# The first projection block of a two-layer decoder trunk traced piece by piece, with its loads issued in the order of their use

## The chip, the cores and the metric

The kernel runs on one core of a Trainium2 chip. The metric is device time in microseconds (us) of one execution; lower is better. The engines are PE (TensorE, the matrix multiplier; PEld is its weight load), DVE (VectorE), ACT (ScalarE), POOL (GpSimd) and SP (SyncE, which here only issues DMA transfers).

## The reference

The input is x, 256 tokens by 2048 channels, float32. Layer 0 mixes tokens by a gated linear recurrence (HGRN2), layer 1 by a gated spatial MLP; after each mixer stands a gated feed-forward network with a short causal convolution. Every sub-layer ends in `x = LayerNorm(ALPHA * x + sublayer(x))`. The part that matters here is the very first projection:

```python
proj = x @ w_in                       # (256 x 2048) @ (2048 x 8192)
q, f, i, g = split(proj)              # 2048 columns each
q = silu(q)
```

The first block of the kernel computes the first 512 columns of q, out of the whole of x and 512 columns of w_in.

## The kernel before

**Splitting.** Every matmul operand that needs float32 accuracy is held as two tiles, hi (the value rounded to fp32r) and lo (the remainder). A product takes hi times hi, hi times lo and lo times hi. For an activation tile X both halves lie side by side, 256 columns each, so that in `block_b` one matmul of 512 columns (`both`, L159: weight hi against X hi and X lo) and one of 256 columns (`rest`, L166: weight lo against X hi) do one product of 128 rows by 128 columns. Such a couple is called a pair below.

**Weights.** `plan` lists all weight chunks in the order of use. A chunk is 512 by 512 floats (1 MB, four slices of 128 rows). `fetch` (L73) issues its load on SP into one of three `raw` buffers; `convert` (L83) makes `whi` with ACT (L93) and `wlo` with DVE (L94), by default in two halves of two slices. `chunk` keeps up to AHEAD = 3 chunks in progress. A load into a `raw` buffer waits until the chunk three places earlier has been converted.

**The first block.** x lies in memory by tokens and has to be turned: `turn(t, k0, n)` (L299) transposes n slices of 128 channels of token tile t on PE into `pt`, copies them to X hi with ACT and subtracts with DVE into X lo (both L317). Two PSUM buffers serve all `pt` tiles. The main program walks over XSEQ: five pieces of x, of 2, 2, 4, 4 and 4 slices of 128 channels. For each piece it issues the load of x, the load of a weight chunk (the first one in four pieces of 256 KB, all four ahead of the second piece of x), then the two turns, under `tc.high_priority()`, and then the conversion of the chunk, ordered after the turns by `issue_after`. Only then does `hgrn` begin, whose first `block_b` call writes the matmuls: 4 chunks of 16 pairs, for each slice k of x four pairs j = 0 to 3 into four PSUM tiles `pb`. In the last chunk the pairs run by j.

**What sets the order.** A scheduler in the recording layer merges all this into one fixed sequence for each engine when the program is built: an earlier place in the program gives priority, `high_priority()` raises it, `issue_after` is a lower bound. On the chip each engine works through its sequence and waits on semaphores.

In the text below, x0 to x4 are the five pieces of x, and chunk 0 to chunk 3 the four weight chunks of the first block. x0 and x1 belong to chunk 0, and x2, x3, x4 to chunks 1, 2, 3.

Of the kernel before, what the change touches and what calls it, by code (L numbers as in the profile page):

```python
# [8 lines left out]
F32 = mybir.dt.float32  # L9
# [6 lines left out]
P = 128  # L16
S = 256
D = 2048
NK = D // P
# [6 lines left out]
NB = 512  # L26
CK = 4
# [3 lines left out]
AHEAD = 3  # L31
# [2 lines left out]
PAD_LO = 128  # L34
PAD1 = 224
BLOCK = {1: 32, 4: 32, 16: 64}
XSEQ = ((0, 2, 4), (2, 2, 0), (4, 4, 1), (8, 4, 1), (12, 4, 0))
TURN_ACT = 3


class Trunk:
# [28 lines left out]
    def want(self, w, k0, c0, extra=False):  # L70
        self.plan.append((w, k0, c0, extra))

    def fetch(self, pieces=1):  # L73
        w, k0, c0, extra = self.plan[self.issued]
        self.issued += 1
        raw = self.wp.tile([P, CK, NB], F32, tag="raw", name="raw")
        src = w[k0 * P : (k0 + CK) * P, c0 : c0 + NB].rearrange("(k p) n -> p k n", p=P)
        n = CK // pieces
        for i in range(0, CK, n):
            self.nc.sync.dma_start(raw[:, i : i + n, :], src[:, i : i + n, :])  # L80
        return raw, extra

    def convert(self, raw, extra, pieces=2):  # L83
        nc = self.nc
        pool = self.xp if extra else self.wp
        hi = pool.tile([P, CK, NB], F32R, tag="hi", name="whi")
        if not extra:
            pool.tile([P, PAD_LO], mybir.dt.uint8, tag="gap", name="gap", bufs=1)
        lo = pool.tile([P, CK, NB], F32R, tag="lo", name="wlo")
        n = CK // pieces  # L90
        for i in range(0, CK, n):
            s = slice(i, i + n)
            nc.scalar.copy(hi[:, s, :], raw[:, s, :])  # L93
            self.last_lo = nc.vector.tensor_tensor(  # L94
                lo[:, s, :], raw[:, s, :], hi[:, s, :].bitcast(F32), ALU.subtract
            )
        self.ready.append((hi, lo))

    def ahead(self, n):
        while self.issued < min(self.taken + n, len(self.plan)):  # L100
# [46 lines left out]
            for t in range(2):  # L147
                evac(t, ps[t])

    def block_b(self, act, w, nch, c0, evac, halves=False):  # L150


        nc = self.nc
        ps = [self.acc.tile([P, 2, S], F32, tag="acc", name="pb") for _ in range(4)]
        last = nch * CK - 1

        def both(ch, k, j, s=slice(0, S), start=True):
            c = slice(j * P, (j + 1) * P)
            nc.tensor.matmul(  # L159
                ps[j][:, :, s], ch[0][:, k % CK, c], act[:, k, :, s],  # L160
                start=start and k == 0, stop=k == last, skip_group_check=halves,
            )

        def rest(ch, k, j):
            c = slice(j * P, (j + 1) * P)
            nc.tensor.matmul(  # L166
                ps[j][:, 1, :], ch[1][:, k % CK, c], act[:, k, 0, :],
                start=False, stop=False, skip_group_check=halves,
            )

        def one(ch, k, j):
            for m in (rest, both) if k else (both, rest):
                m(ch, k, j)

        first = 0
        if halves:
            first = nch
            held = [self.chunk(w, ci * CK, c0) for ci in range(nch)]
            for t in range(2):
                for k in range(last):  # L180
                    for j in range(4):
                        both(held[k // CK], k, j, slice(t * P, (t + 1) * P), t == 0)
            for k in range(last):
                for j in range(4):
                    rest(held[k // CK], k, j)
            for j in range(4):
                one(held[-1], last, j)
        for ci in range(first, nch):
            ch = self.chunk(w, ci * CK, c0)
            ks = range(ci * CK, (ci + 1) * CK)  # L190
            if ci < nch - 1:
                order = [(k, j) for k in ks for j in range(4)]
            else:
                order = [(k, j) for j in range(4) for k in ks]
            for k, j in order:
                one(ch, k, j)
        for j in range(4):
            evac(j, ps[j])

    def gather(self, pool, ps, out):  # L200

        nc = self.nc
        r = pool.tile([P, S], F32, tag="rest", name="rest")
        nc.scalar.copy(r, ps[:, 1, :])  # L204
        nc.vector.tensor_tensor(out, ps[:, 0, :], r, ALU.add)
# [212 lines left out]
    def masks(self, h1):  # L418
# [25 lines left out]
        for i in range(4):  # L444
            s = slice(32 * i, 32 * i + 32)
            nc.gpsimd.tensor_copy(self.diag[s], self.ident[s, s])

    def hgrn(self):
        nc, tc = self.nc, self.tc
        w = self.a["hg_w_in"][0]  # L450
        with ExitStack() as st:
            hp = st.enter_context(tc.tile_pool(name="hp", bufs=1))
            lp = st.enter_context(tc.tile_pool(name="lp", bufs=2))
            h1 = st.enter_context(tc.tile_pool(name="h1", bufs=1))
            self.load_vectors(h1.tile([P, 8, P], F32, tag="o", name="rows"))
            self.masks(h1)
            scores = []
            for i in range(2):
                sc = [
                    h1.tile([P, *n], F32, name=f"{name}{i}")  # L460
                    for name, n in (("scores", (3, 2, P)), ("near32", (4, 32)), ("near64", (4, 64)))
                ]
                for s in sc:
                    nc.gpsimd.memset(s, 0.0)
                scores.append(sc)
            for g in range(4):
                self.hgrn_group(g, w, hp, lp, h1, scores)

    def hgrn_group(self, g, w, hp, lp, h1, scores):
        nc = self.nc  # L470
        q = hp.tile([P, 4, S], F32, tag="q", name="q")
# [5 lines left out]
        def ev_silu(dst):  # L477
            def ev(j, ps):
                self.gather(lp, ps, dst[:, j, :])
                r = lp.tile([P, S], F32, tag="sig", name="sig")  # L480
                nc.scalar.activation(r, dst[:, j, :], AF.Sigmoid)
                nc.vector.tensor_tensor(dst[:, j, :], dst[:, j, :], r, ALU.mult)

            return ev
# [10 lines left out]
        def ev_v(t, ps):  # L495
            nc.scalar.copy(v[:, t, :], ps)

        self.block_b(self.X, w, 4, 0 * D + g * NB, ev_silu(q))
        if g == 0:
            self.vectors()  # L500
            self.bounds(h1)
# [12 lines left out]
        for half in range(2):  # L514
            ps = self.misc.tile([P, 2, 2, P], F32, tag="m", name="po")
            for t in range(2):
                for hh in range(2):
                    i = half * 4 + t * 2 + hh
# [4 lines left out]
            for hh in range(2):  # L523
                j = 2 * half + hh
# [308 lines left out]
@with_exitstack  # L833
def tile_trunk(ctx: ExitStack, tc: tile.TileContext, *args):
    a = dict(zip(_INS, args))
    out = args[len(_INS)]
    k = Trunk(ctx, tc, a)
    nc = tc.nc
    k.plan_hgrn()
    k.plan_ffn(0)  # L840
    k.plan_gmlp()
    k.plan_ffn(1)
    k.constants()
    for k0, n, pieces in XSEQ:
        k.load_x(k0, n)
        chunk = k.fetch(pieces) if pieces else None
        with tc.high_priority():
            for t in range(2):
                hi, lo = k.turn(t, k0, n)
        if chunk:  # L850
            with tc.issue_after(hi.ins), tc.issue_after(lo.ins):
                k.convert(*chunk, pieces=max(pieces, 2))
    k.hgrn()

    def store(t, c):
        s = slice(c * NB, (c + 1) * NB)
        nc.sync.dma_start(out[0, t * P : (t + 1) * P, s], k.z[:, t, s])

    k.hgrn_out()
    k.ffn(0)  # L860
    k.xps.close()
    k.gmlp()
    k.ffn(1, store)
    k.xps.close()
    k.ln.close()
# [32 lines left out]
```

## Time and profile before

| what | value |
|---|---|
| three runs | 2281.47 us median (2280.64 to 2282.81) |
| the profiled execution: its own time | 2282.26 us |
| its span in the trace | 2280.6 us |
| PE busy in the span | 2258.8 us, 12781 matmuls |
| DVE, ACT busy | 1473.4 us, 1105.4 us |
| bytes read from memory | 425.98 MB, 188 GB/s over the span |
| first matmul of the first block, first one of the second block | 9.83 us, 36.99 us from the span's start |

The span runs from the first to the last recorded instruction; the run's own time is 1.7 us longer. An engine's busy time says little alone: what counts is which engine the chain of work that ended last runs through, and where that engine stands idle. In a timeline, the number in brackets is the idle time ahead of a row and the name behind the arrow what ended it. Neighbouring matmuls overlap in the records, since the end of one is drawn after the start of the next; their pace is read from the distance of their starts.

### The profile page before, as it was taken

Reading aid. Unit: us, or ns where it says so; the run is one execution under the profiler, and the core shown is the slowest. Engines: PE = TensorE matmul, PEld = TensorE weight load, DVE = VectorE, ACT = ScalarE, POOL = GpSimd, SP = SyncE. Lnnn points to the kernel's source line nnn. Section 1 sums busy time; section 2 is a strip of 40 time slices with the busy share of each in tenths; the row PEclk is TensorE's granted clock in tenths of the full one; section 3 lists DMA queues with packets and bytes.
Section 4 is the critical chain, followed back from the end, with each engine's and each line's share of the span. In section 5 each row is a group of like instructions: output and inputs, shape, how many; then the busy total and the mean of one; then the engine's idle time right before and its main releaser. Section 6 shows DMA issues by size and latency. Waiting matters only on the chain.

```text
span 2280.6 us, 31751 instructions
## 1 busy us (share of the span) xinstructions
PE 2258.8 (99%) x12781; PEld 1925.7 (84%) x12781; DVE 1473.4 (65%) x2327; ACT 1105.4 (48%) x1698; POOL 48.5 (2%) x102
## 2 busy tenths in 40 slices
PE   8999999999999999999999999999999999999998
PEld 7888888889888888888888888888888888888886
DVE  5777677667665665456666676566765666465655
ACT  5666565545443444344444545455444444344542
POOL 3000000000000000000000000000000000000000
PEclk9999999999999999999999999999999999999999
DMA  7454645645565555555555676655565555555563
GB/s 260 151 181 140 198 149 167 206 166 200 186 227 196 186 185 187 199 186 185 187 196 175 208 218 183 230 177 181 185 234 180 196 186 193 193 185 187 183 203 111
DMA packets 214052, 430.14 MB, mean 189 GB/s; under 512 B 7544, under 2 KB 8336, under 8 KB 213904
## 3 DMA queue, kind: packets, MB, share of 16 engines
q1 hardware_dynamic: 209536, 415.26, 54.5%
q0 software_dynamic: 4368, 12.85, 1.9%
q8 instruction: 100, 1.64, 0.3%
q14 instruction: 48, 0.39, 0.0%
HBM read 425.98 MB, written 2.10 MB: 188 GB/s over the span
## 4 chain that ended last, share of the span: by engine, by line
PE 97%; DVE 2%; ACT 1%; DMA 0%; issue 0%; SPq 0%; DVEq 0%; ACTq 0%
PE pb L159 38%; PE pb L166 20%; PE pa L123 12%; PE pa L125 12%; PE pa L124 12%; DVE wlo L94 1%; PE pl L550 1%; PE pt L305 1%; ACT whi L93 0%; PE pg L752 0%; PE pa L673 0%; PE pa L675 0%; PE pa L674 0%; DMA z<-in_x_dram 0%; PE po L522 0%; PE pout L642 0%
## 5 line engine op out<-in xcount | busy, mean ns | idle before, releaser
L94 DVE TENSOR_TENSOR wlo<-raw,whi 128x1024 fp32r<-128x1024 f32 (+1 forms) x786 | 930.6, 1219 | 693.3 <-ACT whi L93 684.9
L159 PE MATMUL pb<-X,whi 128*128 128x512 f32 (+1 forms) x3960 | 1335.1, 388 | 1.9 <-DVE X L317 1.9
L93 ACT CAST whi<-raw 128x1024 fp32r<-128x1024 f32 (+1 forms) x786 | 790.2, 1047 | 894.8 <-PE pb L159 418.7
L166 PE MATMUL pb<-X,wlo 128*128 128x256 f32 x3840 | 1049.7, 281 | 0.0
L159 PEld LDWEIGHTS pb<-X,whi 128*128 128x128 f32 x3960 | 725.0, 188 | 160.1 <-DVE X L317 2.3
L166 PEld LDWEIGHTS pb<-X,wlo 128*128 128x128 f32 x3840 | 715.7, 189 | 6.1
L123 PE MATMUL pa<-whi,Y 128*128 128x512 f32 x928 | 365.4, 394 | 0.0
L125 PE MATMUL pa<-whi,Y 128*128 128x512 f32 x928 | 363.5, 392 | 0.0
L124 PE MATMUL pa<-wlo,Y 128*128 128x512 f32 x928 | 361.2, 389 | 0.0
L125 PEld LDWEIGHTS pa<-whi,Y 128*128 128x128 f32 x928 | 173.9, 187 | 40.4
L124 PEld LDWEIGHTS pa<-wlo,Y 128*128 128x128 f32 x928 | 174.3, 188 | 37.8
L123 PEld LDWEIGHTS pa<-whi,Y 128*128 128x128 f32 x928 | 174.9, 188 | 35.6
L204 ACT COPY rest<-pb 128x256 f32<-128x256 f32 x240 | 87.9, 369 | 110.9 <-PE pb L159 92.9
L123 PE MATMUL pa<-whi,X 128*128 128x512 f32 x256 | 101.8, 398 | 0.0
L124 PE MATMUL pa<-wlo,X 128*128 128x512 f32 x256 | 101.4, 396 | 0.0
L125 PE MATMUL pa<-whi,X 128*128 128x512 f32 x256 | 100.6, 393 | 0.0
L803 DVE SCALAR_TENSOR_TENSOR act<-a,cols,act 128x254 f32<-128x254 f32 (+1 forms) x176 | 73.2, 481 | 0.0
L125 PEld LDWEIGHTS pa<-whi,X 128*128 128x128 f32 x256 | 48.1, 188 | 11.8
L123 PEld LDWEIGHTS pa<-whi,X 128*128 128x128 f32 x256 | 48.1, 188 | 11.4
L124 PEld LDWEIGHTS pa<-wlo,X 128*128 128x128 f32 x256 | 48.2, 188 | 10.6
L397 DVE TENSOR_TENSOR z<-z,pa 128x512 f32<-128x512 f32 x40 | 27.4, 684 | 34.5 <-PE pa L125 30.3
L807 ACT ACTIVATE act<-act 128x256 f32<-128x256 f32 x88 | 33.8, 415 | 8.7 <-DVE act L803 8.5
(164 smaller groups left out, 1033.2 us busy)
## 6 DMA issues: line engine op xcount, KB each, us to landing
raw<-in_ffn_w_up_dram SPq DMA_DIRECT2D x176, 1024.0 KB, 4.9
raw<-in_ffn_w_down_dram SPq DMA_DIRECT2D x88, 1024.0 KB, 4.9
raw<-in_hg_w_in_dram SPq DMA_DIRECT2D x63, 1024.0 KB, 5.1
raw<-in_sg_w_in_dram SPq DMA_DIRECT2D x32, 1024.0 KB, 5.5
raw<-in_hg_w_out_dram SPq DMA_DIRECT2D x16, 1024.0 KB, 4.9
raw<-in_sg_w_out_dram SPq DMA_DIRECT2D x16, 1024.0 KB, 4.9
g<-in_ln_g_dram POOLq DMA_DIRECT2D x16, 256.0 KB, 6.5
b<-in_ln_b_dram POOLq DMA_DIRECT2D x16, 256.0 KB, 8.8
```

The source lines that it names most:

```text
L93: nc.scalar.copy(hi[:, s, :], raw[:, s, :])
L94: self.last_lo = nc.vector.tensor_tensor(lo[:, s, :], raw[:, s, :], hi[:, s, :].bitcast(F32), ALU.subtract)
L123: nc.tensor.matmul(ps[t], xh, hi[:, kk, :], start=n[t] == 0, stop=False)
L124: nc.tensor.matmul(ps[t], xh, lo[:, kk, :], start=False, stop=False)
L125: nc.tensor.matmul(ps[t], xl, hi[:, kk, :], start=False, stop=last)
L159: nc.tensor.matmul(ps[j][:, :, s], ch[0][:, k % CK, c], act[:, k, :, s], start=start and k == 0, stop=k == last, skip_group_check=halves,)
L166: nc.tensor.matmul(ps[j][:, 1, :], ch[1][:, k % CK, c], act[:, k, 0, :], start=False, stop=False, skip_group_check=halves,)
L204: nc.scalar.copy(r, ps[:, 1, :])
L305: nc.tensor.transpose(ps[:, j, :], self.z[:, t, k * P : (k + 1) * P], self.ident)
L397: nc.vector.tensor_tensor(zz, zz, ps, ALU.add)
L803: nc.vector.scalar_tensor_tensor(cv[:, d:], x[:, : S - d], self.c(("cw", l, 2 - d), f), cv[:, d:], ALU.mult, ALU.add,)
L807: nc.scalar.activation(cv, cv, AF.Silu)
```

## The change

The main loop over XSEQ becomes a method `start`. `fetch` and `convert` are cut into a part that allocates and a function that does one piece, so that both can be called piece by piece. SP now issues x0, two slices of chunk 0, x1, the other two slices of chunk 0, and then x2, chunk 1, x3, chunk 2, x4. The turns of a piece lose `high_priority()` and get a lower bound instead: not before the matmuls of the first half of the piece before. The conversions still follow the turns of their piece. The matmuls of chunks 0 to 2 are written right behind the turns and conversions of each piece, instead of in `block_b`, which is left with chunk 3 (`begun`).

```diff
-XSEQ = ((0, 2, 4), (2, 2, 0), (4, 4, 1), (8, 4, 1), (12, 4, 0))
+XSEQ = ((0, 2), (2, 2), (4, 4), (8, 4), (12, 4))
...
+    def start(self):
+
+        tc = self.tc
+        self.load_x(*XSEQ[0])
+        first, load = self.begin_fetch()
+        load(0, 1)
+        load(1, 1)
+        self.load_x(*XSEQ[1])
+        load(2, 1)
+        load(3, 1)
+        raw = [first]
+        for x in XSEQ[2:]:
+            self.load_x(*x)
+            if len(raw) < 3:
+                raw.append(self.fetch())
+        ps = self.begun = self.begin_b()
+        last = None
+        for i, (k0, n) in enumerate(XSEQ):
+            with tc.issue_after(last.ins) if last else nullcontext():
+                for t in range(2):
+                    hi, lo = self.turn(t, k0, n)
+            c = k0 // CK
+            if c == 3:
+                break
+            if k0 % CK == 0:
+                step = self.begin_convert(*raw[c])
+            with tc.issue_after(hi.ins), tc.issue_after(lo.ins):
+                for m in range(0, n, n // 2):
+                    step(k0 % CK + m, n // 2)
+            for k in range(k0, k0 + n):
+                for j in range(4):
+                    ch = self.ready[c]
+                    if k:
+                        self.rest(ps, self.X, ch, k, j)
+                    m = self.both(ps, self.X, ch, k, j, NK - 1)
+                    if not k:
+                        m = self.rest(ps, self.X, ch, k, j)
+                if k == k0 + n // 2 - 1:
+                    last = m
+        self.ready = self.ready[3:]
+        self.taken = 3
+        with tc.issue_after(hi.ins), tc.issue_after(lo.ins):
+            self.ahead(AHEAD)
...
-        self.block_b(self.X, w, 4, 0 * D + g * NB, ev_silu(q))
+        self.block_b(self.X, w, 4, 0 * D + g * NB, ev_silu(q), begun=self.begun if g == 0 else None)
...
-    for k0, n, pieces in XSEQ:
-        k.load_x(k0, n)
-        chunk = k.fetch(pieces) if pieces else None
-        with tc.high_priority():
-            for t in range(2):
-                hi, lo = k.turn(t, k0, n)
-        if chunk:
-            with tc.issue_after(hi.ins), tc.issue_after(lo.ins):
-                k.convert(*chunk, pieces=max(pieces, 2))
+    k.start()
```

The sequences that come out of the scheduler differ in the first 174 instructions of PE, 41 of DVE, 37 of ACT and 7 of SP; behind these they are the same, and POOL's is the same throughout. Three places show it. In the rows a name carries a buffer number: `pt_90` and `pt_102` are turned pieces of x, `pb_261` to `pb_264` (before) and `pb_98` to `pb_101` (now) the four PSUM tiles of the first block.

PE, from the turn of x1 to the turn of x2, before (`pt_112`, `pt_117` are x1, `pt_125`, `pt_132` x2; `whi_100`, `wlo_102` are chunk 0):

```order
L305 MATMUL pt_112<-ident_76,z_71 128x128 x2
L305 MATMUL pt_117<-ident_76,z_71 128x128 x2
L159 MATMUL pb_261<-X_68,whi_100 128x512
L159 MATMUL pb_262<-X_68,whi_100 128x512
L166 MATMUL pb_261<-X_68,wlo_102 128x256
L166 MATMUL pb_262<-X_68,wlo_102 128x256
L159 MATMUL pb_263<-X_68,whi_100 128x512
L166 MATMUL pb_263<-X_68,wlo_102 128x256
L159 MATMUL pb_264<-X_68,whi_100 128x512
L166 MATMUL pb_264<-X_68,wlo_102 128x256
L305 MATMUL pt_125<-ident_76,z_71 128x128 x4
L305 MATMUL pt_132<-ident_76,z_71 128x128 x4
```

PE now, at the end of the second slice of x0 and the turn of x1 (`pt_135`, `pt_140`; chunk 0 is `whi_112`, `wlo_114`):

```order
L218 MATMUL pb_100<-X_68,wlo_114 128x256
L211 MATMUL pb_100<-X_68,whi_112 128x512
L218 MATMUL pb_101<-X_68,wlo_114 128x256
L211 MATMUL pb_101<-X_68,whi_112 128x512
L328 MATMUL pt_135<-ident_76,z_71 128x128 x2
L328 MATMUL pt_140<-ident_76,z_71 128x128 x2
L218 MATMUL pb_98<-X_68,wlo_114 128x256
L211 MATMUL pb_98<-X_68,whi_112 128x512
```

The turn of x1 stood ahead of all matmuls; now it stands behind the eight pairs of x0 and right ahead of the first pair that reads what it turns.

PE now, at the border of chunk 0 and chunk 1 (x2 is `pt_165`, `pt_172`; chunk 1 is `whi_179`, `wlo_181`):

```order
L218 MATMUL pb_101<-X_68,wlo_114 128x256
L211 MATMUL pb_101<-X_68,whi_112 128x512
L328 MATMUL pt_165<-ident_76,z_71 128x128 x4
L328 MATMUL pt_172<-ident_76,z_71 128x128 x4
L218 MATMUL pb_98<-X_68,wlo_181 128x256
L211 MATMUL pb_98<-X_68,whi_179 128x512
```

Before, the turn of x2 stood twelve pairs of chunk 0 ahead of the first pair that reads it (the last two rows of the first piece); now no pair lies between. The borders of chunks 1 and 2 and of chunks 2 and 3 look the same, `pt_218` and `pt_225` (x3), `pt_271` and `pt_278` (x4) in their places.

ACT now, with its waits, around the turn of x2:

```order
L340 CAST X_68<-pt_135 128x2x128 [waits PE_49]
L340 CAST X_68<-pt_140 128x2x128 [waits PE_49]
L105 CAST whi_112<-raw_85 128x512 [waits DMAHW4_49]
L105 CAST whi_112<-raw_85 128x512 [waits DMAHW5_49]
L340 CAST X_68<-pt_165 128x4x128 [waits PE_49]
L340 CAST X_68<-pt_172 128x4x128 [waits PE_49]
L105 CAST whi_179<-raw_92 128x1024 [waits DMAHW7_49]
```

On ACT nothing moved in this stretch: as before, the copies of a piece of x stand ahead of the conversion of its chunk. DVE has the same order of pieces.

## Rows read from the trace of the kernel before

**Rows 1.** The page: busy time by engine, and the shares of the chain that ended last by engine.

```profile
PE 2258.8 (99%) x12781; PEld 1925.7 (84%) x12781; DVE 1473.4 (65%) x2327; ACT 1105.4 (48%) x1698; POOL 48.5 (2%) x102
PE 97%; DVE 2%; ACT 1%; DMA 0%; issue 0%; SPq 0%; DVEq 0%; ACTq 0%
```

**Rows 2.** What PE waited for over the whole span: us in total, times, the longest in us.

```profile
PE pt L305 <- DMA z<-in_x_dram: 8.0, 2, 4.3
PE pb L159 <- DVE X L317: 1.9, 2, 1.1
PE pl L550 <- DVE W L581: 0.7, 4, 0.2
PE pv L274 <- DVE cols L275: 0.5, 1, 0.5
PE po L522 <- DVE o L519: 0.2, 1, 0.2
```

**Rows 3.** Timeline of PE, first 39 us and one later place (at 504.85 eight transposes and the matmul behind them): start, duration, engine, line, operation.

```profile
4.30 1.09 PE L305 MATMUL pt<-ident,z 128*128 128x128 f32 x4 [4.30 <-DMA z<-in_x_dram]
...
9.09 1.09 PE L305 MATMUL pt<-ident,z 128*128 128x128 f32 x4 [3.70 <-DMA z<-in_x_dram]
...
11.26 0.63 PE L159 MATMUL pb<-X,whi 128*128 128x512 f32 x1
...
11.90 0.63 PE L159 MATMUL pb<-X,whi 128*128 128x512 f32 x1
...
15.40 0.60 PE L305 MATMUL pt<-ident,z 128*128 128x128 f32 x4
...
19.03 0.42 PEld L305 LDWEIGHTS pt<-ident,z 128*128 128x128 f32 x4 [0.36 <-DVE X L317]
...
24.14 0.39 PE L159 MATMUL pb<-X,whi 128*128 128x512 f32 x1
...
34.89 0.39 PE L159 MATMUL pb<-X,whi 128*128 128x512 f32 x1
...
36.85 0.35 PE L274 MATMUL pv<-ident,rows 128*128 128x128 f32 x2
36.99 0.48 PE L159 MATMUL pb<-X,whi 128*128 128x512 f32 x1
...
38.34 0.32 PE L274 MATMUL pv<-ident,rows 120*128 120x120 f32 x1 [0.52 <-DVE cols L275]
...
504.85 1.09 PE L305 MATMUL pt<-ident,z 128*128 128x128 f32 x8
505.69 0.48 PE L673 MATMUL pa<-whi,Y 128*128 128x512 f32 x1
```

**Rows 4.** Busy time of each engine (instructions) from the turn of x1 to the end of the first block, with the granted clock, the share of the DMA engines and GB/s.

```profile
9.09:36.85 27.76, 27.69 (x156) 24.46 (x157) 18.77 (x24) 17.67 (x26) 16.25 (x36) 1.00 0.90 318
```

**Rows 5.** The chain that ended last, in its first 15 us: start, length, what.

```profile
3.22 5.74 DMA z<-in_x_dram
...
12.10 0.43 PE pb L159
12.53 0.21 PE pb L166
...
14.27 0.24 PE pb L159
```

**Rows 6.** Timeline of ACT, turns and conversions of x0, x1 and x2.

```profile
5.00 0.80 ACT L317 CAST X<-pt 128x256 fp32r<-128x256 f32 x2 [2.91 <-PE pt L305]
5.69 1.14 ACT L93 CAST whi<-raw 128x512 fp32r<-128x512 f32 x2
9.79 0.80 ACT L317 CAST X<-pt 128x256 fp32r<-128x256 f32 x2 [2.96 <-PE pt L305]
10.48 1.14 ACT L93 CAST whi<-raw 128x512 fp32r<-128x512 f32 x2
13.63 1.14 ACT L317 CAST X<-pt 128x512 fp32r<-128x512 f32 x2 [2.00 <-PE pt L305]
14.66 2.00 ACT L93 CAST whi<-raw 128x1024 fp32r<-128x1024 f32 x2
```

**Rows 7.** Timeline of DVE in the same stretch.

```profile
5.40 0.85 DVE L317 TENSOR_TENSOR X<-pt,X 128x256 fp32r<-128x256 f32 x2 [5.40 <-ACT X L317]
6.35 1.29 DVE L94 TENSOR_TENSOR wlo<-raw,whi 128x512 fp32r<-128x512 f32 x2
...
11.14 1.29 DVE L94 TENSOR_TENSOR wlo<-raw,whi 128x512 fp32r<-128x512 f32 x2
14.25 1.29 DVE L317 TENSOR_TENSOR X<-pt,X 128x512 fp32r<-128x512 f32 x2 [1.81 <-ACT X L317]
15.75 1.23 DVE L94 TENSOR_TENSOR wlo<-raw,whi 128x1024 fp32r<-128x1024 f32 x1 [0.21 <-ACT whi L93]
16.89 1.42 DVE L94 TENSOR_TENSOR wlo<-raw,whi 128x1024 fp32r<-128x1024 f32 x1
```

**Rows 8.** DMA issues of SP in narrow windows, us from issue to landing behind the size: chunk 1 (issued at 4.21), chunk 2 (5.57), x4 (6.61) and chunk 3, whose issue in SP's timeline stands ahead of it.

```profile
raw<-in_hg_w_in_dram SPq DMA_DIRECT2D x1, 1024.0 KB, 9.1
raw<-in_hg_w_in_dram SPq DMA_DIRECT2D x1, 1024.0 KB, 12.3
z<-in_x_dram SPq DMA_DIRECT2D x1, 512.0 KB, 12.3
12.46 0.37 SPq L80 DMA_DIRECT2D raw<-in_hg_w_in_dram  x1
raw<-in_hg_w_in_dram SPq DMA_DIRECT2D x1, 1024.0 KB, 8.9
```

**Rows 9.** Busy time by engine at the end of the span, where PE has nothing left to do: window, its length, PE, PEld, DVE, ACT, POOL (instructions), granted clock of PE, DMA share, GB/s.

```profile
2269.00:2270.00 1.00, 1.00 (x6) 0.74 (x4) 0.00 (x0) 0.00 (x0) 0.00 (x0) 1.00 0.00 0
2270.00:2271.00 1.00, 0.31 (x2) 0.00 (x0) 0.65 (x1) 0.00 (x0) 0.00 (x0) 1.00 0.00 0
...
2273.00:2274.00 1.00, 0.00 (x0) 0.00 (x0) 1.00 (x2) 0.00 (x0) 0.00 (x0) 0.67 0.00 0
2274.00:2275.00 1.00, 0.00 (x0) 0.00 (x0) 1.00 (x3) 0.00 (x0) 0.00 (x0) 0.50 0.00 0
```

More of the change, by code (lines that the diff above doesn't have):

```diff
@@ L71, in want, with fetch, begin_fetch @@
         self.plan.append((w, k0, c0, extra))
-    def fetch(self, pieces=1):
+    def fetch(self):
+        (raw, extra), load = self.begin_fetch()
+        load(0, CK)
+        return raw, extra
+    def begin_fetch(self):
         w, k0, c0, extra = self.plan[self.issued]
@@ L77, in fetch, with load, begin_convert @@
         src = w[k0 * P : (k0 + CK) * P, c0 : c0 + NB].rearrange("(k p) n -> p k n", p=P)
-        n = CK // pieces
-        for i in range(0, CK, n):
+        def load(i, n):
             self.nc.sync.dma_start(raw[:, i : i + n, :], src[:, i : i + n, :])
-        return raw, extra
+        return (raw, extra), load
     def convert(self, raw, extra, pieces=2):
+        step = self.begin_convert(raw, extra)
+        for i in range(0, CK, CK // pieces):
+            step(i, CK // pieces)
+    def begin_convert(self, raw, extra):
         nc = self.nc
@@ L89, in convert, with step @@
         lo = pool.tile([P, CK, NB], F32R, tag="lo", name="wlo")
-        n = CK // pieces
-        for i in range(0, CK, n):
+        self.ready.append((hi, lo))
+        def step(i, n):
             s = slice(i, i + n)
@@ L96, in convert @@
             )
-        self.ready.append((hi, lo))
+        return step
     def ahead(self, n):
@@ L148, in block_a, with block_b @@
                 evac(t, ps[t])
-    def block_b(self, act, w, nch, c0, evac, halves=False):
+    def block_b(self, act, w, nch, c0, evac, halves=False, begun=None):
         nc = self.nc
-        ps = [self.acc.tile([P, 2, S], F32, tag="acc", name="pb") for _ in range(4)]
+        ps, first = begun or self.begin_b(), 0
+        if begun:
+            first = self.taken
         last = nch * CK - 1
         def both(ch, k, j, s=slice(0, S), start=True):
[L158 to L162, printed above, removed]
-        def rest(ch, k, j):
[L165 to L169, printed above, removed]
+            self.both(ps, act, ch, k, j, last, s, start, halves)
+        def rest(ch, k, j):
+            self.rest(ps, act, ch, k, j, halves)
         def one(ch, k, j):
@@ L173, in one @@
                 m(ch, k, j)
-        first = 0
         if halves:
@@ L198, in block_b, with begin_b, both, rest @@
             evac(j, ps[j])
+    def begin_b(self):
+        return [self.acc.tile([P, 2, S], F32, tag="acc", name="pb") for _ in range(4)]
+    def both(self, ps, act, ch, k, j, last, s=slice(0, S), start=True, loose=False):
+        c = slice(j * P, (j + 1) * P)
+        return self.nc.tensor.matmul(
+            ps[j][:, :, s], ch[0][:, k % CK, c], act[:, k, :, s],
+            start=start and k == 0, stop=k == last, skip_group_check=loose,
+        )
+    def rest(self, ps, act, ch, k, j, loose=False):
+        c = slice(j * P, (j + 1) * P)
+        return self.nc.tensor.matmul(
+            ps[j][:, 1, :], ch[1][:, k % CK, c], act[:, k, 0, :],
+            start=False, stop=False, skip_group_check=loose,
+        )
     def gather(self, pool, ps, out):
```

## The prediction

> **What bounds the kernel now.** I read the page first. PE is busy for 99% of the span and carries 97% of the chain that ended last [rows 1], so time can only be won where PE stands still. The list of PE's waits has 8.0 us for x before the first and the second turn, and little over 3 us in all the rest [rows 2]. The change touches the first block alone, so next I read PE's timeline there. PE turns x0 at 4.30, stands still from 5.39 for 3.70 us until x1 has landed, turns x1 at 9.09 and then works almost without a break until the second block begins at 36.99 [rows 3]: 27.69 of 27.76 us are busy [rows 4]. The wait at 9.09 also shows that the order of the sequence binds. The first pairs need only x0 and slice 0, and their operands were there long before: ACT's conversion of slice 0 ends at 5.69 + 1.14/2 = 6.26 [rows 6], DVE's X lo of x0 at 5.40 + 0.85 = 6.25 and wlo of slice 0 near 7.0 [rows 7]. PE did not take them up because the turn of x1 stood ahead of them and waited for its DMA, which took 5.74 us from 3.22 to 8.96 [rows 5].
>
> The pace of PE has two levels in this stretch. A pair takes 11.90 - 11.26 = 0.64 us early on, and (34.89 - 24.14)/31 = 0.347 us later [rows 3]. The 512-column matmul takes 0.43 us at 12.10 and 0.24 at 14.27 [rows 5], so PE runs at 1.2 GHz until about 13.2 and then at 2.4 GHz, although the granted clock reads 1.00 over the whole stretch [rows 4]. From 9.09 to 13.2 are 4.1 us at half pace, which cost about 2.05 us.
>
> **The change part by part.** As the sequences behind the first block are unchanged and PE is the bound there, I compare when PE ends the first block. The work is the same, 64 pairs and 28 transposes after x0's turn; what differs is the start and the holes.
>
> *Start.* The first pair now follows the turn of x0. It can begin when X lo (6.25) and whi of slice 0 (6.26) are ready, at about 6.35 with a tenth for the semaphore. Unbroken work began at 9.09: 2.74 us gained. The wait of 0.36 us at 19.03 for a turn's PSUM buffer [rows 3] goes as well. The 4.1 us at half pace I take as in the run before, so the eight pairs of x0 end near 11.0. What is late next is the turn of x1.
>
> *Hole at x1.* The turn of x1 now stands directly ahead of the first pair that needs its result. Behind it comes a chain through ACT and DVE that lay under other work or under the DMA wait before. Four quick transposes take 0.60 us with the drain of the last [rows 3], two about 0.38, so ACT begins 0.43 after the turn does. From ACT's first copy to the end of wlo of the slice: ACT 9.79 [rows 6], DVE conversion from 11.14, first half 0.65 [rows 7], which is 2.00 us. With a tenth for the semaphore PE goes on 2.5 us after the turn began, of which its transposes use 4 x 0.11 = 0.45. The hole is 2.05 us.
>
> *Holes at x2, x3, x4.* Each is of one form: eight transposes (505.69 - 504.85 = 0.84 us of PE's time), ACT begins 0.65 us after the first (0.60 and a little). From there the old chain can be read whole: ACT's copy begins at 13.63 and its conversion at 14.66 [rows 6]; DVE's first wlo half begins at 15.75, set free by ACT's whi, and ends at 16.98 [rows 7]. That is 3.35 us, and PE goes on 0.65 + 3.35 + 0.1 = 4.1 us after the turn began. Less the 0.84 of its own work the hole is 3.26 us, three times 9.8 us. The second half of a conversion costs nothing: DVE ends it 1.3 us after the first, while PE has eight pairs, 2.8 us, to do. ACT cannot take the conversion of chunk 1 up early, although its data land at 4.21 + 9.1 = 13.3 [rows 8]: on ACT it stands behind the copies of x2, these wait for PE's transposes, and these stand behind all pairs of chunk 0. The same lock holds on DVE.
>
> *Loads.* Moving x1 ahead of two slices of chunk 0 makes it land sooner than 8.96, but PE now asks for it only at about 11.0: worth nothing, and the two slices that it passes are wanted after 12 us, by when even the old order had both x1 and them in. Chunk 2 and x4 land at 17.9 and 18.9 [rows 8], wanted at about 26 and 35. The load of chunk 3 waits for the last conversion of chunk 0, now near 14.1 instead of 12.46; with the 8.9 us of before [rows 8] it lands by 23, wanted near 37. All of SP's work lies under at least 3 us of cover. If that cover were gone, each us would lengthen a hole by one.
>
> *Behind the block.* The transposes `pv` of the row vectors begin earlier, three of them inside the last hole. The stall of 0.52 at 38.34 [rows 3] goes, but the third `pb` tile of the second block now waits for an evacuation queued behind DVE's conversions, some 0.2. I take -0.3, with bounds -0.5 and +0.7.
>
> Sum: -2.74 - 0.36 + 2.05 + 9.8 - 0.3 = +8.4 us. The second block should begin near 45.5 instead of 36.99. In the profiled execution that gives 2282.26 + 8.4 = 2290.7; this execution lies 0.8 above the median of the three runs, and from the median it is 2281.47 + 8.4 = 2289.9, which I forecast.
>
> **The clock in the holes.** The trace shows no hole of 2 to 3 us in warm work. The nearest row is the end of the span: PE's last matmul ends at 2270.3, and the granted clock goes from 1.00 to 0.50, that is to 1.2 GHz, a third of the way into 2273 to 2274 [rows 9], 3.0 us after the work ended. From the end of the last transpose PE's long holes last 3.0 us too. So from below a hole costs no clock; from above each of the three drops PE to 1.2 GHz, and if it needs 4.1 us of work to get back as at the start, that costs 2.05 us a time. I take none, because the work returns just as the fall of the end came, and keep the other end for the range. At the start the rise could come later too, as the hole at x1 breaks the work: at worst the other eight pairs of chunk 0 also run at 0.64, 8 x 0.29 = 2.3 us.
>
> The Trainium skill (TensorE: Matmul & The Clock Gate, section HAM oscillation) describes a kernel in which every wait between groups of matmuls throttles PE again, so that every group starts at half rate. By it the sum would be three falls above mine, near 2296. No run here shows it for holes of this length; the end of the span agrees that idleness brings the fall.
>
> **The rivals.**
>
> *Clock falls.* As above: one fall 2291.9, two 2294.0, three 2296.0, a late rise at the start up to 2.3 more. For it: the holes are as long as the stretch in which the end's clock fell. Against it: no longer than that, and the fall need not meet every hole.
>
> *The holes are short.* If the conversions of chunks 1 to 3 ran under the pairs of the chunk before, only the turn itself would be exposed: X lo of x2 ends 14.25 + 1.29 - 13.63 = 1.91 us after ACT's first copy [rows 6, 7], PE could go on after 0.65 + 1.91 + 0.1 = 2.66, a hole of 1.8 less the 0.2 for the `rest` matmul that goes first. At x1 it would be about 1.3. Then -3.4 + 1.3 + 4.8 = +2.7, 2284.2. Against it: ACT's sequence has the copies ahead of the conversion, and ACT's idle time ahead of each copy [rows 6] shows that it waits there.
>
> *Only the start counts.* If PE found other work during a turn's way through ACT and DVE, so that each of the four holes stayed under 0.8 us, the gain of the start (3.4 with the `pv` stall) would outweigh them. Without any hole it is 2278.1. For it: before, the same turns were hidden almost wholly [rows 4]. Against it: there they stood ahead of up to twelve pairs, now of none. The point at which it decides is a mean hole of 0.85 us.
>
> *The loads do it.* That the new order of loads brings x1 early and so sets the time would show in a wait for x1 at PE; with x1 wanted at 11.0 it has nothing to give, and this case falls together with the forecast.
>
> **How the numbers follow.** Forecast, the four holes with a clock that holds: 0.55, 2288.3 to 2291.7 by itself (0.3 us for each of the holes, 0.5 for the rest). Clock falls: 0.33. Short holes: 0.07. Only the start: 0.03. Left for what I don't see: 0.02. The range reaches from 2286.0, between the short holes and the forecast, to 2296.0 with three falls. A measurement of this kernel can tell about 0.2%, 4.6 us, from no change. Forecast and clock falls lie beyond it on the slow side, 0.88; the short holes and the bare start lie within it, 0.10; for more than 4.6 us faster I see no mechanism, 0.02.
>
> **What would show it.** In the profile of the changed kernel: the first pair at about 6.4; PE idle ahead of the pairs at four places, near 11.5 for 2 us and near 17, 27 and 36 for 3.2 us, set free by DVE's wlo; the second block beginning near 45.5; the waits of PE for DVE's wlo some 10 us in all, a line that is not there now. If the 512-column matmuls behind a hole take 0.43 instead of 0.24, the clock fell. I am wrong if PE's waits in the first 50 us stay under 5 us, or if PE does not wait for wlo but for a load.

## The result: 0.46% slower, and the profile after

| | median | lowest to highest | runs |
|---|---|---|---|
| before | 2282.07 us | 2280.64 to 2282.87 | 6 |
| after | 2292.82 us | 2291.39 to 2294.32 | 6 |

The ratio is 1.0046, with a 95% interval from 1.0036 to 1.0057: 8.2 to 13.0 us lost. The forecast was 2289.9, its range 2286.0 to 2296.0. The profiled execution of the changed kernel took 2293.31 us with a span of 2291.6, 11.0 more than the span of before.

On the page, busy time by engine and the shares of the chain that ended last:

```profile
PE 2263.6 (99%) x12781; PEld 1928.1 (84%) x12781; DVE 1473.0 (64%) x2327; ACT 1107.3 (48%) x1698; POOL 47.2 (2%) x102
PE 96%; DVE 2%; ACT 1%; issue 0%; DMA 0%; DVEq 0%; ACTq 0%
```

Beside [rows 1] the same 12781 matmuls keep PE busy 4.8 us longer. A busy time that grows for the same work means that the work ran slower; this is the first sign of the clock. The other 6.2 us of the longer span are idle time. What PE waited for over the whole span, the longest single wait last:

```profile
PE pb L218 <- DVE wlo L106: 8.5, 4, 2.9
PE pt L328 <- DMA z<-in_x_dram: 3.9, 1, 3.9
...
PE pv L297 <- DVE X L340: 1.2, 2, 1.0
```

The first row has no counterpart in [rows 2]: four waits for DVE's `wlo`. In exchange, of the two waits for x only that for x0 is left. The third row is part of the hole at x4, in which transposes of the row vectors `pv` stand. PE's timeline of the first block (start, duration, operation, in brackets the idle time ahead and what ended it):

```profile
6.03 1.62 PE L211 MATMUL pb<-X,whi 128*128 128x512 f32 x3 [1.01 <-ACT whi L105]
...
11.29 0.78 PE L328 MATMUL pt<-ident,z 128*128 128x128 f32 x4
13.83 0.39 PE L218 MATMUL pb<-X,wlo 128*128 128x256 f32 x1 [1.76 <-DVE wlo L106]
...
18.12 1.22 PE L328 MATMUL pt<-ident,z 128*128 128x128 f32 x8
22.28 0.58 PE L218 MATMUL pb<-X,wlo 128*128 128x256 f32 x1 [2.94 <-DVE wlo L106]
...
29.34 1.03 PE L328 MATMUL pt<-ident,z 128*128 128x128 f32 x8
33.31 0.38 PE L218 MATMUL pb<-X,wlo 128*128 128x256 f32 x1 [2.93 <-DVE wlo L106]
...
38.97 1.03 PE L328 MATMUL pt<-ident,z 128*128 128x128 f32 x8
...
42.93 0.58 PE L218 MATMUL pb<-X,wlo 128*128 128x256 f32 x1 [0.85 <-DVE wlo L106]
...
49.66 0.62 PE L211 MATMUL pb<-X,whi 128*128 128x512 f32 x2
```

Four times a turn (L328) stands directly ahead of the first `rest` (L218) that reads its piece, and a hole lies between. The second matmul of the last row, at 49.89, is the first one of the second block, which stood at 36.99 before [rows 3]. From 6.03 to 49.89 the block takes 43.86 us; before, it took 27.90 from the turn of x1 on, at 9.09.

The chain that ended last shows what lies in such a hole. Around x2 it reads (start, length, what; `issue` is time in which the profile shows no wait; L211 is `both`, L340 the copies of a turn, L105 and L106 the two steps of the conversion):

```profile
17.89 0.43 PE pb L211
18.32 0.59 PE pt L328 x4
18.91 0.02 issue
18.94 1.07 ACT X L340 x2
20.01 0.95 ACT whi L105
20.96 0.02 issue
20.99 1.25 DVE wlo L106
22.23 0.04 issue
22.28 0.58 PE pb L218
22.86 0.43 PE pb L211
```

Nothing in it is a DMA: half of the transposes, both copies of ACT, one half of the conversion on ACT, the same half on DVE. These follow each other while PE has nothing else in its sequence. Before, twelve pairs stood there. The last row is the sign that the prediction had set for a fall of the clock: the 512-column matmul behind the hole takes 0.43 us and not 0.24.

The granted clock of PE, in windows of 1 us (window, length, PE, PEld, DVE, ACT, POOL with their instructions, granted clock, DMA share, GB/s):

```profile
14.00:15.00 1.00, 1.00 (x7) 0.86 (x8) 0.39 (x1) 0.00 (x0) 0.87 (x3) 1.00 1.04 395
15.00:16.00 1.00, 1.00 (x5) 0.90 (x4) 0.00 (x0) 0.00 (x0) 0.97 (x1) 0.54 1.06 403
18.00:19.00 1.00, 1.00 (x8) 0.88 (x7) 0.00 (x0) 0.06 (x1) 0.87 (x5) 0.76 1.05 403
...
21.00:22.00 1.00, 0.00 (x0) 0.00 (x0) 1.00 (x1) 0.90 (x1) 1.00 (x3) 0.95 0.01 2
22.00:23.00 1.00, 0.72 (x2) 0.72 (x3) 1.00 (x2) 0.00 (x0) 0.96 (x2) 0.50 0.00 0
...
25.00:26.00 1.00, 1.00 (x7) 0.90 (x6) 0.00 (x0) 0.00 (x0) 0.41 (x2) 0.84 0.92 246
...
33.00:34.00 1.00, 0.69 (x4) 0.65 (x5) 1.00 (x2) 0.00 (x0) 0.00 (x0) 1.00 0.00 0
...
42.00:43.00 1.00, 0.15 (x2) 0.07 (x1) 1.00 (x2) 1.00 (x2) 0.00 (x0) 0.69 0.00 0
43.00:44.00 1.00, 1.00 (x4) 0.90 (x5) 1.00 (x2) 1.00 (x2) 0.00 (x0) 0.50 0.00 0
45.00:46.00 1.00, 1.00 (x6) 0.91 (x5) 1.00 (x2) 1.00 (x2) 0.00 (x0) 0.60 0.84 213
```

Three stretches run at 0.50, that is 1.2 GHz: shortly after 15 to about 18.5, from 21.9 to a third into 25, and from 42.4 to 45.8. Behind the hole at x3 the clock stays at 1.00. Before, it read 1.00 over the whole block [rows 4].

With a pair at 0.347 us and a transpose at 0.105 at full pace (0.84 us for eight), as in the prediction, the 43.86 us divide as follows:

| part | us | from |
|---|---|---|
| 64 pairs and 28 transposes at full pace | 25.2 | 64 x 0.347 + 28 x 0.105 |
| hole at x1 | 2.1 | 13.83 - 11.29 - 0.45 |
| holes at x2, x3, x4 | 9.6 | 4.16 + 3.97 + 3.96 from turn to `rest`, less 3 x 0.84 |
| half pace at the start | 2.5 | 11.29 - 6.03, less 8 x 0.347 |
| half pace behind x1, x2, x4 | 4.5 | 4.29 for 8 pairs, 7.06 and 6.96 for 16 each, chunk 2 with 5.66 adds 0.1 |

### The profile page after: what moved, and what is told of

Same layout as the page of the kernel before. It is cut to its first block, busy times and chain, and to the rows that moved or that the text cites. A ratio compares the mean times of both kernels' runs of the same rounds, so it can differ in the third digit from the quotient of the medians.

```text
span 2291.6 us, 31752 instructions
## 1 busy us (share of the span) xinstructions
PE 2263.6 (99%) x12781; PEld 1928.1 (84%) x12781; DVE 1473.0 (64%) x2327; ACT 1107.3 (48%) x1698; POOL 47.2 (2%) x102
## 4 chain that ended last, share of the span: by engine, by line
PE 96%; DVE 2%; ACT 1%; issue 0%; DMA 0%; DVEq 0%; ACTq 0%
PE pb L211 38%; PE pb L218 20%; PE pa L136 12%; PE pa L138 12%; PE pa L137 12%; DVE wlo L106 1%; PE pl L617 1%; ACT whi L105 1%; PE pt L328 0%; PE pg L819 0%; PE pa L740 0%; PE pa L742 0%; PE pa L741 0%; PE po L589 0%; ACT X L340 0%
## 5 line engine op out<-in xcount | busy, mean ns | idle before, releaser
L106 DVE TENSOR_TENSOR wlo<-raw,whi 128x1024 fp32r<-128x1024 f32 (+1 forms) x786 | 930.1, 1219 | 685.0 <-ACT whi L105 676.5
L211 PE MATMUL pb<-X,whi 128*128 128x512 f32 (+1 forms) x3960 | 1338.3, 389 | 2.9 <-DVE X L340 1.9
L105 ACT CAST whi<-raw 128x1024 fp32r<-128x1024 f32 (+1 forms) x786 | 791.9, 1050 | 885.2 <-PE pb L211 410.8
L218 PE MATMUL pb<-X,wlo 128*128 128x256 f32 x3840 | 1050.2, 281 | 8.5 <-DVE wlo L106 8.5
L211 PEld LDWEIGHTS pb<-X,whi 128*128 128x128 f32 x3960 | 726.7, 188 | 162.2 <-DVE X L340 2.3
L218 PEld LDWEIGHTS pb<-X,wlo 128*128 128x128 f32 x3840 | 717.4, 189 | 15.8 <-DVE wlo L106 9.4
```

What stands on the lines that cost most here:

```text
L106: self.last_lo = nc.vector.tensor_tensor(lo[:, s, :], raw[:, s, :], hi[:, s, :].bitcast(F32), ALU.subtract)
L211: return self.nc.tensor.matmul(ps[j][:, :, s], ch[0][:, k % CK, c], act[:, k, :, s], start=start and k == 0, stop=k == last, skip_group_ch ...
L218: return self.nc.tensor.matmul(ps[j][:, 1, :], ch[1][:, k % CK, c], act[:, k, 0, :], start=False, stop=False, skip_group_check=loose,)
```

## The experiments

The theory after the result: the four holes come from the place of the turns (each directly ahead of its first use, with the conversion of its chunk locked behind its copies), the clock falls follow from the holes, and the order of the loads gives and takes nothing. The rivals: the loads or something behind the block; or holes that any order would have. In each comparison the kernel before ran on the same chip: 2282.34 us in the first four experiments and 2282.14 in the others, 27 runs each. Ratios are against these.

### e1: the turns taken earlier again

```diff
             with tc.issue_after(last.ins) if last else nullcontext():
-                for t in range(2):
-                    hi, lo = self.turn(t, k0, n)
+                with tc.high_priority():
+                    for t in range(2):
+                        hi, lo = self.turn(t, k0, n)
```

> The changed kernel with high_priority() put back around the turns, their lower bound kept. In the sequence of PE the turn of x1 then stands four pairs ahead of its first use, that of x2 four pairs, those of x3 and x4 eight. Theory (the place of the turns makes the holes): the holes shrink to about 0, 1.9, 0.5 and 0.5 us from 2.1, 3.3, 3.1 and 3.1, and the clock stays up in them; with the earlier start of 3 us left over the time is about 2281.5, near the kernel before (2282.1). Rival (the piecewise writing or the order of the loads costs the time, not the turns): 2290 to 2293, as the changed kernel.

Measured: 2281.01 us (2279.38 to 2281.89), ratio 0.9994, interval 0.9985 to 1.0003. One line takes all of the loss away. PE's timeline at x2:

```profile
12.80 1.03 PE L328 MATMUL pt<-ident,z 128*128 128x128 f32 x8
...
16.77 0.39 PE L218 MATMUL pb<-X,wlo 128*128 128x256 f32 x1 [1.54 <-DVE wlo L106]
```

The turn of x2 now begins at 12.80, ahead of pairs of chunk 0, and what follows it takes the same 4 us as in the changed kernel (12.80 to 16.77), but a hole of only 1.5 us is left of it; at the other three, by the starts of the matmuls, at most 0.3. The granted clock stays at 1.00. The chain through ACT and DVE is not shorter. It is covered.

### e2: still earlier

```diff
+        bound = {2: 0, 4: 1, 8: 4, 12: 8}
+        done = {}
         for i, (k0, n) in enumerate(XSEQ):
+            last = done[bound[k0]] if k0 else None
...
-                if k == k0 + n // 2 - 1:
-                    last = m
+                done[k] = m
```

This comes on top of e1's edit: the turn of a piece may begin behind the first slice of the piece before, and that of x2 behind slice 1.

> As the run with high_priority() back, with the lower bounds moved one step earlier: x1 after slice 0, x2 after slice 1, x3 after the first slice of chunk 1, x4 after the first slice of chunk 2. Theory: holes of about 0, 0.5, 0 and 0 us, and the start of 3 us earlier is kept: about 2279 (2278 to 2280.5). Rival (the start was never worth 3 us, since the time is lost again at the second block): 2281.5 to 2282.5, as before.

Measured: 2278.9 us (2278.13 to 2280.77), ratio 0.9987, interval 0.9978 to 0.9996. PE's timeline:

```profile
5.82 1.62 PE L211 MATMUL pb<-X,whi 128*128 128x512 f32 x3 [1.01 <-ACT whi L105]
...
15.91 0.39 PE L218 MATMUL pb<-X,wlo 128*128 128x256 f32 x1 [0.28 <-DVE wlo L106]
...
34.44 0.35 PE L297 MATMUL pv<-ident,rows 128*128 128x128 f32 x2
```

The early start is kept and the hole at x2 is down to 0.28. The pair of `pv` transposes that ends the first block stands at 34.44, against 36.85 before [rows 3]: 2.4 us of the 3.3 that the first pair begins earlier (5.82 against 9.09). This version beats both kernels. Against the one before it gains 3.4 us of 2282: the interval leaves out no change, but the gain is below 0.2%.

### e3: the holes left, PE kept at work in them

```diff
+        zero = self.Y[:, 0, 0, :P]
+        self.nc.gpsimd.memset(zero.bitcast(F32), 0.0)
...
+            if last:
+                for f in range(4 if n == 2 else 12):
+                    self.nc.tensor.matmul(
+                        ps[f % 4], zero, self.X[:, 0, :, :],
+                        start=False, stop=False, skip_group_check=True,
+                    )
```

The added matmuls, behind each turn, multiply by zero and add nothing to the sums.

> The changed kernel with matmuls of a zero tile added behind each turn (4 at x1, 12 at each of the others, 0.21 us each at 2.4 GHz), which add zeros to the block's sums and wait for nothing. The holes stay, PE is busy in them. Theory (holes cost about 11.7 us by themselves and the falls of the clock 4.5 us more): the granted clock stays at 1.00 behind x2, x3 and x4, and the time is about 2288.5 (2287.5 to 2290). Rival (the low clock costs nothing, because the chain through ACT and DVE sets the pace): 2292.8, unchanged.

Measured: 2289.59 us (2289.11 to 2292.74, 5 runs), ratio 1.0038, interval 1.0026 to 1.0051, which overlaps that of the changed kernel. Three of the five runs took 2289.1 to 2289.6 at a mean granted clock of 0.999; the two others took 2292.7, like the changed kernel, at 0.997 and 0.998. In the runs of the changed kernel it is 0.995 to 0.997. The trace is of one of the three, 2289.11, and in it the clock reads 1.00 over the whole block. PE's timeline at x2 and x3:

```profile
15.28 1.03 PE L328 MATMUL pt<-ident,z 128*128 128x128 f32 x8
...
19.25 0.39 PE L218 MATMUL pb<-X,wlo 128*128 128x256 f32 x1 [0.15 <-DVE wlo L106]
...
28.89 0.38 PE L218 MATMUL pb<-X,wlo 128*128 128x256 f32 x1 [0.16 <-DVE wlo L106]
```

From turn to `rest` it is still 3.97 us, but the 28.89 - 19.25 = 9.64 us of a chunk are now 16 x 0.347 of pairs, 0.84 of transposes and 3.25 of hole, without any clock loss. In the changed kernel the first chunk behind a long hole took 33.31 - 22.28 = 11.03. So the falls of the clock come on top of the holes, and work in the holes can keep them away: the profiled execution is 4.2 us shorter than that of the changed kernel (2289.11 against 2293.31), beside 4.5 us at half pace in the table. The two do not match in every part: the start took 1.1 us less here and a later wait of PE for DVE's `y` 1.6 us more. Why two runs took the full 2292.7 is not known; no trace of them was kept.

### e4: the conversions of chunks 1 and 2 ahead of the turns

```diff
+            c = k0 // CK
+            if c in (1, 2):
+                step = self.begin_convert(*raw[c])
+                with tc.issue_after(hi.ins), tc.issue_after(lo.ins):
+                    for m in range(0, n, n // 2):
+                        step(m, n // 2)
             with tc.issue_after(last.ins) if last else nullcontext():
                 for t in range(2):
                     hi, lo = self.turn(t, k0, n)
...
```

> The changed kernel with the conversions of chunks 1 and 2 written ahead of the turns of x2 and x3, so that ACT and DVE can make them under the pairs of the chunk before; the turns and chunk 3 stay where they are. Theory (two thirds of a hole is the conversion locked in behind the turn's copies): the holes at x2 and x3 shrink from 3.2 us to about 1.8 us, that at x4 stays, the clock falls less often: 2287 to 2290. Rival (only the turn and its copies make the hole, the conversion would have been in time anyway): 2292.8, unchanged.

Measured: 2285.63 us (2284.8 to 2287.04), ratio 1.0016, interval 1.0007 to 1.0025: better than either theory had it. PE's timeline:

```profile
16.22 1.03 PE L328 MATMUL pt<-ident,z 128*128 128x128 f32 x8
17.98 0.73 PE L218 MATMUL pb<-X,wlo 128*128 128x256 f32 x4 [0.73 <-ACT X L340]
18.82 1.19 PE L211 MATMUL pb<-X,whi 128*128 128x512 f32 x4
...
35.79 0.38 PE L218 MATMUL pb<-X,wlo 128*128 128x256 f32 x1 [0.85 <-DVE wlo L106]
```

With the conversion out of the chain, PE goes on after 17.98 - 16.22 = 1.76 us instead of 4.16, and what sets it free is ACT's copy: X hi is enough for the four `rest`, and DVE's X lo comes under them. The hole at x4, left as it was, is still 3.97 us (31.82 to 35.79). In the block the clock did not fall at all (mean 0.999), neither behind the 1.76 us of idleness at x1 nor at x4, which the expectations had not assumed.

### e5: the kernel before, with the new order of loads

```diff
         for i in range(0, CK, n):
+            if pieces == 4 and i == 2:
+                self.load_x(2, 2)
             self.nc.sync.dma_start(raw[:, i : i + n, :], src[:, i : i + n, :])
...
-        k.load_x(k0, n)
+        if k0 != 2:
+            k.load_x(k0, n)
```

> The kernel before with only the order of the first loads changed: x1 issued after two slices of chunk 0 instead of after four. There PE does wait for x1 (until 9.09). Theory: x1 lands near 7.5, the unbroken work begins 1.5 us earlier and the whole is 1.5 us shorter, about 2280.8 (2280 to 2281.8). Rival (the wait only moves to the two slices of chunk 0 that are passed, or to the conversion): 2282.3, unchanged.

Measured: 2281.98 us (2280.61 to 2282.3), ratio 0.9998, interval 0.9989 to 1.0007. The theory missed: x1 did arrive earlier, yet nothing was gained. PE's timeline:

```profile
7.32 1.20 PE L161 MATMUL pb<-X,whi 128*128 128x512 f32 x2
...
15.26 0.63 PE L307 MATMUL pt<-ident,z 128*128 128x128 f32 x4 [2.31 <-DMA z<-in_x_dram]
19.31 0.63 PE L307 MATMUL pt<-ident,z 128*128 128x128 f32 x4 [0.40 <-DMA z<-in_x_dram]
```

The first pairs begin at 7.32, 2.5 us before the 9.83 of the kernel before. But in its sequence turns of the next pieces stand among the early pairs, and at 15.26 and 19.31 PE waits 2.31 and 0.40 for their loads. These are the turns of x3 and x4. Moving x1 brings their loads no sooner: x3 landed at 14.8 before and at 15.1 here, x4 at 18.9 and 19.2. The wait for x1 has become one for later pieces, of about the length of the gain. The order of loads gains nothing there because the order of turns asks for x3 and x4 before they land.

### e6 and e7: the old order of loads, in the changed kernel and in e2

```diff
         load(1, 1)
-        self.load_x(*XSEQ[1])
         load(2, 1)
         load(3, 1)
+        self.load_x(*XSEQ[1])
```

> The changed kernel with the old order of the first loads (x1 after all four slices of chunk 0). Theory: PE asks for x1 only at about 11, so the order is worth nothing there: about 2292.8 (2291.5 to 2294), and no wait for a load at the turn of x1. Rival (the loads carry part of the loss or of the gain): off by 1 us or more either way, with the hole at x1 longer than 2.1 us.

Measured: 2291.74 us (2290.86 to 2293.65, 5 runs), ratio 1.0045, interval 1.0032 to 1.0057, the ratio of the changed kernel (1.0046). From turn to `rest` the four pieces take 2.35, 3.96, 3.96 and 3.96 us; PE doesn't wait for x1. The holes are those of the changed kernel, but the falls of the clock are not. PE's timeline:

```profile
12.80 0.39 PE L218 MATMUL pb<-X,wlo 128*128 128x256 f32 x1 [1.76 <-DVE wlo L106]
13.03 0.40 PE L211 MATMUL pb<-X,whi 128*128 128x512 f32 x1
...
30.88 0.58 PE L218 MATMUL pb<-X,wlo 128*128 128x256 f32 x1 [2.93 <-DVE wlo L106]
31.26 0.63 PE L211 MATMUL pb<-X,whi 128*128 128x512 f32 x1
...
39.31 1.03 PE L328 MATMUL pt<-ident,z 128*128 128x128 f32 x8
```

Behind x1 the work runs at full pace. Behind x2, x3 and x4 the granted clock falls, at x3 for longest: it reads 0.50 from 30.1 to 36.9, and the 16 pairs of chunk 2 take 39.31 - 30.88 = 8.43 us, 2.9 more than at full pace.

> The kernel with the lower bounds of the turns moved earlier (2278.9), with the old order of loads. There PE asks for x1 at 8.5. Theory: x1 lands at about 9, PE waits for it some 0.5 us, which is all the new order is worth: 2279.4 (2278.8 to 2280.5). Rival (order of loads worth nothing in any arrangement): 2278.9 and no wait of PE for x1.

Measured: 2278.82 us (2278.04 to 2279.86), ratio 0.9986, interval 0.9977 to 0.9995, against 0.9987 with the new order. Here the theory missed: x1 landed at 8.5 and its turn stood at 8.69, so the small wait that it expected did not come. In both kernels the new order of loads is worth nothing that can be seen; the intervals leave room for 2 to 3 us, but neither trace has a wait for x1 that could cost them.

### e8: matmuls on zeros ahead of the first turn, in e2

```diff
+        zero = self.Y[:, 0, :, :]
+        self.nc.vector.memset(zero.bitcast(F32), 0.0)
...
+            for f in range(n):
+                self.nc.tensor.matmul(
+                    ps[f % 4], zero[:, 0, :P], zero, start=True, stop=True,
+                )
...
+        warm(4)
...
+            if k0 == 0:
+                warm(2)
```

This comes on top of e2's edit. Four are written ahead of the turn of x0 and two behind it; in PE's sequence all six stand ahead. The first true matmul of each tile overwrites their results.

> The same kernel (2278.9) with six matmuls of a zero tile on PE ahead of the first turn, while x0 is under way, about 1.2 to 3.8 us; their sums are overwritten by the block's first matmuls. Theory (the clock rises after PE has been busy for some us, whatever it computes): the 512-column matmul is down from 0.43 to 0.23 us by about 8 instead of 11 us, 1 to 2.5 us gained: about 2277.2 (2276.3 to 2278.2), faster than the kernel before by over 0.2%. Rival (the low clock of the start lay under waits for data, or the break between x0's turn and the first pair undoes the warming): 2278.9 or a little more.

Measured: 2278.47 us (2277.79 to 2279.34), ratio 0.9985, interval 0.9976 to 0.9994, no gain over e2 that can be told. PE's timeline:

```profile
1.53 2.92 PE L492 MATMUL pb<-Y 128*128 128x512 f32 x6 [1.53 <-DVE Y L488]
...
8.38 0.63 PE L211 MATMUL pb<-X,whi 128*128 128x512 f32 x1
...
10.06 0.40 PE L211 MATMUL pb<-X,whi 128*128 128x512 f32 x1
...
15.96 0.39 PE L218 MATMUL pb<-X,wlo 128*128 128x256 f32 x1 [0.78 <-DVE wlo L106]
```

The full pace came earlier (a matmul takes 0.40 by 10.06; without the zeros, in e7, it still took 0.62 at 11.04). But the first `rest` of chunk 1 stands at 15.96, as in e2 (15.91) and e7 (15.83): there PE waits 0.78 for DVE's `wlo`, and ACT's conversion in front of that began at 13.59, set free by the load of the chunk. So in this execution the load is the next bound of the start, and a faster clock only runs up against it. The zeros also cost something: the turn of x0 begins behind them at 4.25, in e2 at 3.73.

## Why the prediction was right, and where it was not

The sign, the place and the mechanism of the holes were right; e1, e2 and e4 show that mechanism from three sides. The case that the forecast was made for, a clock that holds (2288.3 to 2291.7), did not come: 2292.82 lies among the falls of the clock, between one (2291.9) and two (2294.0). Measured in the profiled execution the loss is 2293.31 - 2282.26 = 11.05 us against the +8.4 of the sum. That it is no further off is in part luck: the clock cost 5.0 us more than the sum had, and the other terms together came out some 2 us lower. Term by term:

*Start: -2.74 forecast, -3.06 measured.* The first pair stands at 6.03 instead of 6.35, as x0 took 3.0 us from issue to landing and not the 3.4 of the run before. In all later runs, with either order of loads, it took 2.8 or 2.9, so this is how the load comes and not the change's doing. The wait of 0.36 for a `pt` buffer is gone as forecast.

*Hole at x1: +2.05 forecast, 2.09 measured. Holes at x2, x3, x4: +9.8 forecast, 9.57 measured.* The step from the turn to the first `rest` was put at 2.5 and 4.1; it took 2.54 and 4.16, 3.97, 3.96. A chain read from the old trace link by link held to within 0.15 us each, since its links are the same instructions in the same order, only without cover. At x4 that it fits is in part chance: there the conversion on DVE began after X lo and the copy of a `pv` result, at 41.70, a path that the sum did not have and that was as long. All holes but a part of that at x4 are ended by DVE's `wlo`, as was said; the waits for it sum to 8.5 and not "some 10", because the transposes drain in the first part of each hole and `pv` stands in the last.

*The clock: "I take none".* This is the step that failed, a term mis-sized at nothing. The table above has 4.5 us at half pace behind holes, and at the start 2.5 us instead of 2.05, together 5.0 more than the sum had. (The start varies by itself: the same eight pairs lost 1.4 us in e3, 2.3 in e4 and 1.8 in e6.) Mainly for this the second block began at 49.89 and not near 45.5. The argument was that work returns just as the end's clock fell, 3.0 us after the last matmul [rows 9]. That row bounds one kind of idleness, one that follows long, unbroken work. Two of the three long holes did bring a fall, x3 did not, and the hole at x1, the shortest, brought one too, 1.3 us after work had come back. The rival "clock falls" was right that it happens. Its 2.05 us a time was too dear for this run, whose three falls cost 1.4 to 1.5 us each, but not for every run: the one behind x3 in e6 cost 2.9. The rule of the Trainium skill that the prediction weighed (TensorE: Matmul & The Clock Gate, section HAM oscillation), a fall at every such wait, is nearer to these runs than my zero: two of three long holes here and all three in e6, but none at x4 in e4, where the hole is as long. e3 shows that work on zeros in the holes can keep the clock up.

*Loads: nothing forecast, nothing found.* e6 and e7 show it in two kernels, by the absence of a wait for x1 and the same ratios. The rival that the loads do it falls.

*Behind the block: -0.3 forecast, -1.1 measured,* outside its bounds. The second block begins 12.9 us later, the next stage (the first matmul of `pd`) 94.81 - 83.03 = 11.78 us later. The stall at 38.34 is gone with a transpose beside it; counted by the starts of the matmuls on both sides of it, the two were worth 0.76 and not 0.52, since the bracket counts only from the drawn end of a matmul. The other side, some 0.2 for an evacuation behind DVE's conversions, did not come: DVE began the additions of the first block's results at 48.47, before the block's end. That leaves about 0.4 not followed.

*The rest of the kernel.* At 504.85 before, 516.55 after, the shift is 11.70; at the end of the span it is 11.0. Where these 0.7 us are won back stays open. So does why the clock held at x3 here and fell there in e6.

The other rivals fall by the timeline: the long holes are not short, as the conversion did stand behind the copies (e4, which frees it, has the 1.8 us from turn to `rest` that X hi alone needs); and "only the start" would have needed holes under 0.85 us. It is e2 that is close to that case: 2278.9, where the prediction had 2278.1 for no hole at all.

## What to carry to other kernels

When the producer of an operand is moved directly ahead of its first use, add up every engine between them as one chain, with all that stands ahead on those engines' sequences: here 4 us a piece, of which PE itself works 0.84. Start work early, but put enough consumers between a producer and its first use to cover its chain: in e1 four pairs at x2 left a hole of 1.5 us, eight at x3 and x4 at most 0.3. A hole in PE's work can cost the clock on top of the hole, so a zero in the sum for that needs a row that shows it, and the range has to carry the fall.

## What the runs showed of the hardware that was not expected

In the changed kernel the granted clock went down to 0.54 in the window of 15 to 16 us, 1.3 us after work had come back from 1.76 us of idleness; 2.93 us of idleness at x3 left it at 1.00. In e4 and e6 the same 1.76 us at x1 brought no fall, and in e6 the same 2.93 us at x3 brought the longest one. The length of the hole alone does not decide, and with the same holes the falls come at other places in another run.

At the start the granted clock reads 1.00 while pairs start 0.64 us apart and not 0.347 (from 9.59 to 10.87), so there the durations tell the pace and the clock's record does not; from 15 us on the two agree.
